# Bias rows copied to DRAM head by head, and SSM constants prepared one stage earlier

## The chip, the cores and the metric

The program runs on one core of one Trainium2 chip. The metric is the device time of the program in microseconds (us), the median of three executions. The core's engines are TensorE (PE, matrix products), VectorE (DVE), ScalarE (ACT) and GpSimd (POOL); SyncE (SP) issues most transfers, ScalarE issues some, and sixteen DMA engines carry them all.

## The reference, cut to what matters

Two residual networks run one after the other on 256 tokens of width 2048, everything in 32-bit floats. The first has two layers: a latent attention (MLA) with its output projection, and a sliding-window attention (SWA) with its output projection. The second mixes an attention with eight heads and a state-space model (SSM), and ends in a feed-forward part.

Two things in it belong to this change. The attention of the second network adds a bias that depends only on the distance between query and key:

```
bias_h = rel_bias.T
lg_own = einsum('bhqd,bhtd->bhqt', qc, k_own) * scale + bias_h[:, t5_bucket(rel_own)]
```

The SSM uses a time step for each of its sixteen heads, projected from the layer's input and passed through a softplus, a decay, and a short convolution in front:

```
xbc = silu(causal_depthwise_conv(xbc, conv_w, conv_b))
dt  = softplus(dt_raw + dt_bias)
a   = -exp(a_log)
a_cs = cumsum(dt * a)
```

## The kernel before

The 256 tokens stand on the free axis and the features on the 128 partitions, so the hidden state is sixteen tiles of 128 x 256 (`KT` = 16). Every large weight lies in DRAM in one packed stream, `wst`, in the order of its use, in pieces of 128 x 1024 floats (512 KB). `fetch` (L285) brings the next piece into one of five `raw` buffers through SyncE's queue. `split_w` (L296) turns it into a high part `whi`, rounded on ScalarE, and a remainder `wlo`, computed on VectorE; four buffers hold each.

`proj` (L326) makes one block of 128 output features: 16 pairs of matmuls, one with `whi` against 512 columns (L336) and one with `wlo` against 256 (L339). A block uses two pieces. `out_mla` (L808) and `out_swa` (L906) run sixteen such blocks each (`j` from 0 to 15), add the residual into `x` and split the new `x` into the operands `hl` of the next stage. `paired` (L343) is a smaller product with both parts of the weights side by side: 16 matmuls at L351. `side` (L360) prepares its weights.

`biases` (L695) is called at block 8 of `out_mla`. It loads a constant (`hot`) and the bias table (`rel`), multiplies them (L706), and keeps the result in `row`, eight partitions of 384 floats, one per head. It loads the time-step weights `wdt`. Last, one transfer on ScalarE's queue writes `row` 128 times into the DRAM tensor `biasrows`, whose order is [128 copies, 8 heads, 384]. Much later the attention reads each head's part back with a skewed pattern, 128 x 256 values a head (L1133).

`mix` (L973) follows `out_swa`. It opens the pool `ssm` and makes there the halved convolution weights `cwh` and `cbh`, the zeroed margins of `pads`, the time-step weights `wdts` (by `side`), then runs `paired` on them; later come `ea` (the exponential of `alog`) and two operands, `acs` and `pick`, for spreading sums over partitions.

The order of instructions on each engine is not that of the code. A planner simulates the engines and gives each engine, at each time, the instruction that is ready and stands earliest in the code; an instruction of later code is taken ahead of time when nothing earlier is ready. It also puts in the waits. Within a pool, a tile waits for the tiles that held its memory before. `with self.tc.manual_schedule(...)` fixes the order by hand in a few places, none of them in the stages of this change.

Of the kernel before, what the change touches and what calls it, by code (L numbers as in the profile page):

```python
# [9 lines left out]
F32 = mybir.dt.float32  # L10
F32R = mybir.dt.float32r
I32 = mybir.dt.int32
AF = mybir.ActivationFunctionType
ALU = mybir.AluOpType
# [3 lines left out]
S = 256  # L18
D = 2048
KT = D // 128  # L20
# [207 lines left out]
class _Kernel:  # L228
# [466 lines left out]
    def biases(self, P):  # L695

        nc = self.nc
        n = 384
        at = _CST["hot"][0]
        hot = P.tile([33, n], F32, name="hot")  # L700
        nc.scalar.dma_start(out=hot, in_=self.cst_dram[0:33, at : at + n])
        rel = P.tile([33, 8], F32, name="rel")
        nc.vector.memset(rel, NEG)
        nc.scalar.dma_start(out=rel[0:32, :], in_=self.rel)
        p = self.aux.tile([128, 512], F32, name="m", bufs=2)
        nc.tensor.matmul(p[:8, :n], rel, hot, start=True, stop=True)  # L706
        row = P.tile([8, n], F32, name="bias")
        self.act(row, p[:8, :n])
        self.wdt = self.const.tile([128, 256], F32, name="wdt")
        nc.scalar.dma_start(out=self.wdt, in_=self.wdt_dram)  # L710
        self.bias = self.tc.dram_tile([128, 8, n], F32, name="biasrows")
        nc.scalar.dma_start(out=self.bias.rearrange("i h n -> h i n"),
                            in_=row.unsqueeze(1).to_broadcast([8, 128, n]))

    def mla(self):
        nc, tc = self.nc, self.tc
# [91 lines left out]
    def out_mla(self):  # L808
        nc = self.nc
        self.xp = self.ctx.enter_context(self.pool("x"))  # L810
        self.x, self.xs, ss = [], [], None
        with self.pool("again") as P:
            for j in range(KT):
                if j == 8:
                    self.biases(P)
                if j == KT - 1:
                    self.roots(self.x[-2])
                if j % 4 == 0:
                    x0 = P.tile([128, 4, S], F32, name="x0", bufs=2)
                    nc.sync.dma_start(out=x0, in_=self.xt[:, j : j + 4, :])  # L820
                x = self.new_x(j)
                self.add2(x, self.proj(self.y), x0[:, j % 4, :])
                self.x.append(x)
                self.xs.append(self.split(self.hx, 16, x, self.v("g2", j)))
                ss = self.square(ss, x)
        self.hy.__exit__(None, None, None)
        self.c2 = self.rstd(self.mean(ss), D, self.const.tile([128, 2], F32, name="c2"))
        self.r2 = self.spread(self.c2)
        for j in range(KT):
            self.dump(f"x1_{j}", self.x[j])  # L830
# [75 lines left out]
    def out_swa(self):  # L906
        nc = self.nc
        gfp = self.const.tile([128, KT], F32, name="gfp")
        self.tt(gfp, self.v("gf", 0, KT), self.v("gpre", 0, KT), ALU.mult)
        old, self.x, self.xs, ss, sg = self.x, [], [], None, None  # L910
        for j in range(KT):
            x = self.new_x(j)
            if j == KT - 1:
                self.roots(self.x[-2])
            self.add2(x, self.proj(self.y), old[j])
            self.x.append(x)
            self.xs.append(self.split(self.hx, 16, x, gfp[:, j : j + 1]))
            ss = self.square(ss, x)
            sg = self.square(sg, x, self.v("gf", j))
        for j in range(KT):  # L920
            self.dump(f"x2_{j}", self.x[j])
        self.hy.__exit__(None, None, None)

        cf = self.rstd(self.mean(ss), D)
        q = self.tmp("n4", (128, 2), 1)
        self.tt(q, self.mean(sg), cf, ALU.mult)
        self.tt(q, q, cf, ALU.mult)
        self.c3 = self.rstd(q, D, self.const.tile([128, 2], F32, name="c3"))
        self.tt(self.c3, self.c3, cf, ALU.mult)
        self.r3 = self.spread(self.c3)  # L930
        self.rf = self.spread(cf)

    def normed(self, j):

        self.stt(self.x[j], self.x[j], self.v("gf", j), self.rf, ALU.mult, ALU.mult)
        self.dump(f"x3_{j}", self.x[j])
# [36 lines left out]
    def mix(self):  # L973
        nc, tc = self.nc, self.tc
        xs = self.xs
        ident = self.k("ident")
# [1 line left out]
        self.hy = self.pool("hy3", side="right")  # L978
        hy = self.hy.__enter__()
        with self.pool("ssm") as P:  # L980
            self.cwh = P.tile([128, 48], F32, name="cwh")
            self.cbh = P.tile([128, 12], F32, name="cbh")
            nc.vector.tensor_scalar(self.cwh, self.v("cw", 0, 48), 0.5, None, op0=ALU.mult)
            nc.vector.tensor_scalar(self.cbh, self.v("cb", 0, 12), 0.5, None, op0=ALU.mult)
            self.pads = [P.tile([128, 3 + S], F32, name=f"pad{i}") for i in range(2)]
            for p in self.pads:
                nc.vector.memset(p[:, 0:3], 0.0)

            sp = [P.tile([128, 32], F32, name=f"sp{i}") for i in range(4)]
            ea = P.tile([128, 16], F32, name="ea")  # L990
            dta = P.tile([128, 2, 16], F32, name="dta")
            ds = P.tile([128, 16], F32, name="ds")
            bc = [P.tile([128, S], F32, name=f"bc{j}") for j in range(2)]
# [1 line left out]
            xd = P.tile([128, 8, 64], F32, name="xd")  # L995


            ws = P.tile([128, KT, 48], F32R, name="wdts")
            nc.vector.memset(ws[:, :, 16:32].bitcast(F32), 0.0)
            self.side(ws, self.wdt, 16)  # L1000
            u = self.tmp("ys")
            self.paired(xs, ws, 16, u)
            self.tt(u[:16], u[:16], self.r3[:16], ALU.mult)
            p = self.aux.tile([128, 512], F32, name="m", bufs=2)
            for t in range(2):
# [4 lines left out]
            for t in range(2):  # L1010
                self.tt(dt[:, t, :], p[:, 16 * t : 16 * t + 16], db, ALU.add)
            self.softplus(sp, dt.rearrange("p a b -> p (a b)"))
            self.act(ea, self.v("alog", 0, 16), AF.Exp)
            for t in range(2):
                self.stt(dta[:, t, :], dt[:, t, :], -1.0, ea, ALU.mult, ALU.mult)

            p = self.aux.tile([128, 512], F32, name="m", bufs=2)
# [9 lines left out]
            p = self.aux.tile([128, 512], F32, name="m", bufs=2)  # L1027
# [1 line left out]
                nc.tensor.matmul(p[:16, 128 * t : 128 * t + 128], dta[:, t, :], self.k("tri"),  # L1029
                                 start=(t == 0), stop=(t == 1), skip_group_check=True)  # L1030

            acs = P.tile([128, S], F32R, name="acs")
            pick = P.tile([128, 16], F32R, name="pick")
            for z in (acs, pick):
                nc.vector.memset(z.bitcast(F32), 0.0)
            self.act(acs[:16], p[:16, :S])
            self.tt(acs[32:48], p[:16, :S], acs[:16].bitcast(F32), ALU.subtract)
            for a in (0, 32):
                nc.vector.tensor_copy(pick[a : a + 16], ident[:16, :16])

            bc += [P.tile([128, S], F32, name=f"bc{j}") for j in (2, 3)]
            for j in range(4):
# [3 lines left out]
            for c in range(2):  # L1046
                for g in range(2):
                    p = self.aux.tile([128, 512], F32, name="m", bufs=2)
# [7 lines left out]
            st, cb = [], []  # L1056
            for g in range(2):
                p = self.aux.tile([128, 512], F32, name="m", bufs=2)
# [4 lines left out]
                p = self.aux.tile([128, 512], F32, name="m", bufs=2)  # L1063
# [4 lines left out]
                p = self.aux.tile([128, 512], F32, name="m", bufs=2)  # L1068
# [10 lines left out]
            for i in range(8):  # L1079
                g = i // 4  # L1080
                y = self.aux.tile([128, 512], F32, name="m", bufs=2)
                for e in range(2):
                    h = 2 * i + e
                    rr = slice(64 * e, 64 * e + 64)
                    a = self.aux.tile([128, 512], F32, name="s", bufs=2)
# [26 lines left out]
                if i % 4 == 3:  # L1112
                    r = self.spread(self.rstd(self.mean(ss), 512),
                                    P.tile([128, S], F32, name=f"rg{g}"))
                    for j in range(4 * g, 4 * g + 4):
                        self.tt(ys[j], ys[j], r, ALU.mult)
                        y_ssm.append(self.split(hy, 8, ys[j], self.v("gssm", j)))


        y_att = []  # L1120
# [2 lines left out]
        with self.pool("att") as P:  # L1123
            n = 384
            rv = self.c3
            for g in range(2):
# [3 lines left out]
                for j in range(4):  # L1130
                    h = 4 * g + j
# [232 lines left out]
```

## Time and profile before

| | |
|---|---|
| median of 3 executions | 1859.26 us (1858.11 to 1861.4) |
| the profiled execution, its own time | 1858.8 us |
| its span, from the first to the last instruction | 1857.0 us |
| mean granted clock of TensorE | 0.995 |
| `out_mla`: PE time, about | 275 to 372 us |
| `out_swa`: PE time, about | 620 to 703 us |
| `mix` begins on PE | 706.24 us |

All times of the trace count from the start of the span. The profiled execution has 1.8 us around its span.

### The profile page before, as it was taken

How to read it: one execution, taken by the hardware profiler on the slowest of the kernel's cores; microseconds unless marked ns; L12 is line 12 of the kernel's file. 1: busy time of each engine (PE TensorE's matmuls, PEld its weight loads, DVE VectorE, ACT ScalarE, POOL GpSimd, SP SyncE). 2: the span in 40 equal slices, each digit the busy share in tenths (PEclk: the TensorE clock that was granted, in tenths of full speed). 3: DMA queues.
4: the chain of work that ended last, by engine and by line, in shares of the span. 5: the costliest groups of instructions: out<-in, count | busy, mean ns of one | idle time of the engine just before them, and what ended most of it. 6: DMA issues, size and time to landing. Idle time of an engine off the chain costs nothing.

```text
span 1857.0 us, 27806 instructions
## 1 busy us (share of the span) xinstructions
PE 1828.4 (98%) x10306; PEld 1572.9 (85%) x10306; DVE 1398.4 (75%) x2578; ACT 1030.2 (55%) x1832; POOL 0.2 (0%) x4
## 2 busy tenths in 40 slices
PE   9999999999999999999999989999999999999997
PEld 8999987898888887888888878888888888888886
DVE  8887776787888677977766578888888888855554
ACT  8655554567777655556554565444444444544543
POOL 0000000000000000000000000000000000000000
PEclk9999999999999999999999999999999999999999
DMA  8544456654444454544454645555555555555553
GB/s 291 176 151 157 148 175 184 215 183 150 144 158 150 158 191 138 182 170 152 149 194 140 206 145 174 181 182 190 184 187 188 184 191 182 196 186 187 202 187 120
DMA packets 92556, 326.13 MB, mean 176 GB/s; under 512 B 10339, under 2 KB 12804, under 8 KB 92420
## 3 DMA queue, kind: packets, MB, share of 16 engines
q1 hardware_dynamic: 89568, 320.49, 50.4%
q10 hardware_dynamic: 2852, 3.86, 1.1%
q8 instruction: 81, 1.33, 0.3%
q14 instruction: 55, 0.45, 0.1%
HBM read 320.64 MB, written 3.67 MB: 175 GB/s over the span
## 4 chain that ended last, share of the span: by engine, by line
PE 94%; DMA 2%; DVE 2%; ACT 1%; issue 1%; SPq 0%; DVEq 0%; ACTq 0%
PE acc L336 44%; PE acc L339 23%; PE acc L1264 4%; PE acc L1265 4%; PE acc L1266 4%; DMA biasrows<-bias 2%; PE acc L469 1%; PE acc L470 1%; PE acc L468 1%; PE m L594 1%; PE acc L450 1%; PE acc L451 1%; PE acc L449 1%; PE m L582 1%; PE s L791 1%
## 5 line engine op out<-in xcount | busy, mean ns | idle before, releaser
L336 PE MATMUL acc<-hl,whi 128*128 128x512 f32 x3584 | 1279.3, 398 | 4.1 <-ACT whi L276 4.1
L339 PE MATMUL acc<-hl,wlo 128*128 128x256 f32 x3584 | 1016.5, 284 | 3.7 <-DVE wlo L270 3.7
L276 ACT ACTIVATE whi<-raw 128x1024 fp32r<-128x1024 f32 (+1 forms) x606 | 628.6, 1041 | 670.3 <-PE acc L336 311.8
L270 DVE TENSOR_TENSOR wlo<-raw,whi 128x1024 fp32r<-128x1024 f32 (+1 forms) x606 | 727.0, 1203 | 352.5 <-ACT whi L276 348.8
L336 PEld LDWEIGHTS acc<-hl,whi 128*128 128x128 f32 x3584 | 674.1, 188 | 161.0 <-ACT whi L276 6.0
L339 PEld LDWEIGHTS acc<-hl,wlo 128*128 128x128 f32 x3584 | 673.8, 188 | 11.8 <-DVE wlo L270 5.2
L1265 PE MATMUL acc<-wlo,hl 128*128 128x512 f32 x344 | 136.1, 397 | 0.0
L1266 PE MATMUL acc<-whi,hl 128*128 128x512 f32 x344 | 135.3, 394 | 0.0
L1264 PE MATMUL acc<-whi,hl 128*128 128x512 f32 x344 | 118.2, 396 | 0.0
L273 DVE SCALAR_TENSOR_TENSOR g<-pad,vec,g 128x256 f32<-128x256 f32 x176 | 84.2, 482 | 2.8
L1265 PEld LDWEIGHTS acc<-wlo,hl 128*128 128x128 f32 x344 | 64.7, 188 | 16.0
L1264 PEld LDWEIGHTS acc<-whi,hl 128*128 128x128 f32 x344 | 64.7, 188 | 15.6
L1266 PEld LDWEIGHTS acc<-whi,hl 128*128 128x128 f32 x344 | 64.7, 188 | 15.2
L270 DVE TENSOR_TENSOR u<-acc,u 128x256 f32<-128x256 f32 x182 | 75.7, 418 | 0.4
L276 ACT ACTIVATE u<-acc 128x256 f32<-128x256 f32 x184 | 67.2, 366 | 5.7 <-DVE q L270 2.8
L276 ACT ACTIVATE t<-t,nm 128x128 f32<-128x128 f32 x112 | 49.4, 444 | 2.3 <-DVE nm L545 1.4
L270 DVE TENSOR_TENSOR t<-s,cst 128x384 f32<-128x384 f32 (+1 forms) x64 | 32.8, 520 | 20.0 <-PE s L890 12.8
L469 PE MATMUL acc<-wlo,hl 128*128 128x512 f32 (+1 forms) x128 | 47.1, 368 | 0.0
L470 PE MATMUL acc<-whi,hl 128*128 128x512 f32 (+1 forms) x128 | 47.1, 368 | 0.0
L468 PE MATMUL acc<-whi,hl 128*128 128x512 f32 (+1 forms) x128 | 46.8, 368 | 0.0
L451 PE MATMUL acc<-hl,wlo 128*128 128x256 f32 x160 | 45.7, 285 | 0.0
L449 PE MATMUL acc<-hl,whi 128*128 128x256 f32 x160 | 45.5, 284 | 0.0
(294 smaller groups left out, 1652.7 us busy)
## 6 DMA issues: line engine op xcount, KB each, us to landing
raw<-in_wst_dram SPq DMA_DIRECT2D x593, 512.0 KB, 3.3
x<-in_xt_dram SPq DMA_DIRECT2D x7, 512.0 KB, 6.0
raw<-in_wst_dram SPq DMA_DIRECT2D x8, 256.0 KB, 6.1
biasrows<-bias ACTq DMA_DIRECT2D x1, 1536.0 KB
b<-biasrows ACTq DMA_DIRECT2D x8, 128.0 KB, 2.8
gb<-in_gfpost_dram ACTq DMA_DIRECT2D x2, 512.0 KB, 4.7
out_dram<-f SPq DMA_DIRECT2D x4, 256.0 KB, 2.3
out_dram<-hl SPq DMA_DIRECT2D x4, 256.0 KB, 2.5
```

The lines of the kernel that those rows point to most:

```text
L270: self.nc.vector.tensor_tensor(out=out, in0=a, in1=b, op=op)
L273: self.nc.vector.scalar_tensor_tensor(out=out, in0=a, scalar=s, in1=b, op0=op0, op1=op1)
L276: self.nc.scalar.activation(out, in_, func, **kw)
L336: nc.tensor.matmul(acc.rearrange("p a t -> p (a t)"), hi[:, a : a + 128], xs[k].rearrange("p a t -> p (a t)"), start=(k == 0), stop=False, ...
L339: nc.tensor.matmul(acc[:, 0, :], lo[:, a : a + 128], xs[k][:, 0, :], start=False, stop=(k == n - 1), skip_group_check=True)
L451: nc.tensor.matmul(acc[:, 0, :], lo[:, a : a + 128], x[:, 0, :], start=False, stop=(k == 3))
L468: nc.tensor.matmul(o, xh, hi[:, a : a + n], start=(k == 0), stop=False)
L469: nc.tensor.matmul(o, xh, lo[:, a : a + n], start=False, stop=False)
L470: nc.tensor.matmul(o, xl, hi[:, a : a + n], start=False, stop=(k == last))
L1264: nc.tensor.matmul(o, xh, hi[:, w], start=(k == 0), stop=False)
L1265: nc.tensor.matmul(o, xh, lo[:, w], start=False, stop=False)
L1266: nc.tensor.matmul(o, xl, hi[:, w], start=False, stop=(k == NF - 1))
```

## The change

The transfer that writes `row` to DRAM becomes eight transfers, one for each head, in a function `copies`. `biases` is called at block 3 of `out_mla` instead of 8, and `copies` at blocks 4 to 11. The preparation of `wdts`, `ea`, `cwh`, `cbh`, `pads`, `acs` and `pick` moves out of `mix` into a function `ssm_ready`, which is called at block 5 of `out_swa`; their tiles come from a pool `ready`, opened before the blocks of `out_swa` and closed after the SSM part of `mix`. The arithmetic is the same.

```diff
@@ biases
-        nc.scalar.dma_start(out=self.bias.rearrange("i h n -> h i n"),
-                            in_=row.unsqueeze(1).to_broadcast([8, 128, n]))
+        return row
+
+    def copies(self, row, h):
+        n = row.shape[1]
+        self.nc.scalar.dma_start(out=self.bias[:, h : h + 1, :].rearrange("i h n -> h i n"),
+                                 in_=row[h : h + 1].unsqueeze(1).to_broadcast([1, 128, n]))
@@ out_mla
-                if j == 8:
-                    self.biases(P)
+                if j == 3:
+                    row = self.biases(P)
+                if 4 <= j < 12:
+                    self.copies(row, j - 4)
@@ out_swa
+        self.ready = self.pool("ready")
+        R = self.ready.__enter__()
         for j in range(KT):
+            if j == 5:
+                self.ssm_ready(R)
@@ new function
+    def ssm_ready(self, P):
+        nc = self.nc
+        self.wdts = P.tile([128, KT, 48], F32R, name="wdts")
+        nc.vector.memset(self.wdts[:, :, 16:32].bitcast(F32), 0.0)
+        self.side(self.wdts, self.wdt, 16)
+        self.ea = P.tile([128, 16], F32, name="ea")
+        self.act(self.ea, self.v("alog", 0, 16), AF.Exp)
+        self.cwh = P.tile([128, 48], F32, name="cwh")
+        self.cbh = P.tile([128, 12], F32, name="cbh")
+        nc.vector.tensor_scalar(self.cwh, self.v("cw", 0, 48), 0.5, None, op0=ALU.mult)
+        nc.vector.tensor_scalar(self.cbh, self.v("cb", 0, 12), 0.5, None, op0=ALU.mult)
+        self.pads = [P.tile([128, 3 + S], F32, name=f"pad{i}") for i in range(2)]
+        for p in self.pads:
+            nc.vector.memset(p[:, 0:3], 0.0)
+        self.acs = P.tile([128, S], F32R, name="acs")
+        self.pick = P.tile([128, 16], F32R, name="pick")
+        for z in (self.acs, self.pick):
+            nc.vector.memset(z.bitcast(F32), 0.0)
+        for a in (0, 32):
+            nc.vector.tensor_copy(self.pick[a : a + 16], self.k("ident")[:16, :16])
@@ mix: the same lines leave the pool "ssm"; what stays is
+            ea, acs, pick = self.ea, self.acs, self.pick
...
-            self.paired(xs, ws, 16, u)
+            self.paired(xs, self.wdts, 16, u)
...
+        self.ready.__exit__(None, None, None)
```

## Rows read from the trace of the kernel before

**Rows 1.** The page: busy time, share of the span and instructions of each engine.
```profile
PE 1828.4 (98%) x10306; PEld 1572.9 (85%) x10306; DVE 1398.4 (75%) x2578; ACT 1030.2 (55%) x1832; POOL 0.2 (0%) x4
```
**Rows 2.** Timeline of PE in `out_mla`: start, us, instruction [idle before, releaser].
```profile
295.61 0.39 PE L336 MATMUL acc<-hl,whi 128*128 128x512 f32 x1
295.84 0.28 PE L339 MATMUL acc<-hl,wlo 128*128 128x256 f32 x1
295.96 0.40 PE L336 MATMUL acc<-hl,whi 128*128 128x512 f32 x1
...
299.75 0.51 PE L336 MATMUL acc<-hl,whi 128*128 128x512 f32 x1 [2.93 <-ACT whi L276]
301.01 0.58 PE L339 MATMUL acc<-hl,wlo 128*128 128x256 f32 x1 [0.75 <-DVE wlo L270]
...
303.95 0.44 PE L336 MATMUL acc<-hl,whi 128*128 128x512 f32 x1
...
320.24 0.39 PE L339 MATMUL acc<-hl,wlo 128*128 128x256 f32 x1 [0.68 <-DVE wlo L270]
```
**Rows 3.** Stretches after both stops: length, busy PE PEld DVE ACT POOL, clock, DMA.
```profile
706.20:711.20 5.00, 4.96 (x15) 2.54 (x16) 1.30 (x4) 0.81 (x3) 0.00 (x0) 0.66 0.29 105
...
299.70:303.90 4.20, 3.40 (x10) 2.69 (x11) 3.24 (x5) 2.07 (x4) 0.00 (x0) 0.61 0.81 233
```
**Rows 4.** Timeline of ScalarE and VectorE in `out_mla` around the copy.
```profile
279.83 0.30 ACTq L712 DMA_DIRECT2D biasrows<-bias  x1
...
280.51 1.41 DVE L270 TENSOR_TENSOR x<-acc,x 128x256 f32<-128x256 f32 x4
...
298.64 1.06 ACT L276 ACTIVATE whi<-raw 128x1024 fp32r<-128x1024 f32 x1 [11.35 <-DMA raw<-in_wst_dram]
```
**Rows 5.** DMA, 288 to 292 us: packets, MB, engine share; issues, us to landing.
```profile
q10 hardware_dynamic: 132, 0.20, 46.7%
q1 hardware_dynamic: 57, 0.23, 17.6%
...
raw<-in_wst_dram SPq DMA_DIRECT2D x2, 512.0 KB, 17.0
```
**Rows 6.** DMA, 304 to 308 us.
```profile
q1 hardware_dynamic: 176, 0.63, 38.7%
q10 hardware_dynamic: 119, 0.18, 25.8%
```
**Rows 7.** Timeline at the start of `mix`.
```profile
703.46 0.18 DVE L983 TENSOR_SCALAR cwh<-vec 128x48 f32<-128x48 f32 x1
...
705.68 0.41 DVE L270 TENSOR_TENSOR wdts<-wdt,wdts 128x256 fp32r<-128x256 f32 x1
...
706.24 5.19 PE L351 MATMUL acc<-hl,wdts 128*48 128x512 f32 x15 [3.51 <-DVE wdts L270]
706.38 0.48 DVE L273 SCALAR_TENSOR_TENSOR hl<-x,gfp,hl 128x256 fp32r<-128x256 f32 x1
```
**Rows 8.** The chain that ended last, the same helper in the MLA stage.
```profile
56.90 3.66 PE acc L351 x16
```
**Rows 9.** Stretch before `out_swa`, columns as in rows 3.
```profile
620.00:630.00 10.00, 10.00 (x63) 8.34 (x63) 2.28 (x4) 3.47 (x6) 0.00 (x0) 1.00 0.32 105
```
**Rows 10.** DMA, 1850 to 1857 us: the final stores.
```profile
DMA packets 864, 1.57 MB, mean 225 GB/s; under 512 B 96, under 2 KB 96, under 8 KB 864
...
q1 hardware_dynamic: 864, 1.57, 62.7%
```
**Rows 11.** Transfers of `wdt` and `hot`: duration ns min/median/max, first and last start.
```profile
L710 ACTq DMA_DIRECT2D wdt<-in_wdt_dram x1: 384/384/384, 1.2 to 1.2; - x1
...
L701 ACTq DMA_DIRECT2D hot<-in_cst_dram x1: 558/558/558, 255.6 to 255.6; - x1
```
**Rows 12.** The final stores, second half of them: issue times and landing.
```profile
L1302 SPq DMA_DIRECT2D out_dram<-hl x4: 333/333/333, 1851.5 to 1853.4; - x4
...
DMA to landing us min/median/max: 2.3/2.4/2.6
```

More of the change, by code (lines that the diff above doesn't have):

```diff
@@ L980, in mix @@
         with self.pool("ssm") as P:
[L981 to L987, printed above, removed]
             sp = [P.tile([128, 32], F32, name=f"sp{i}") for i in range(4)]
-            ea = P.tile([128, 16], F32, name="ea")
+            ea, acs, pick = self.ea, self.acs, self.pick
             dta = P.tile([128, 2, 16], F32, name="dta")
@@ L995, in mix @@
             xd = P.tile([128, 8, 64], F32, name="xd")
-            ws = P.tile([128, KT, 48], F32R, name="wdts")
-            nc.vector.memset(ws[:, :, 16:32].bitcast(F32), 0.0)
-            self.side(ws, self.wdt, 16)
             u = self.tmp("ys")
-            self.paired(xs, ws, 16, u)
+            self.paired(xs, self.wdts, 16, u)
             self.tt(u[:16], u[:16], self.r3[:16], ALU.mult)
@@ L1012, in mix @@
             self.softplus(sp, dt.rearrange("p a b -> p (a b)"))
-            self.act(ea, self.v("alog", 0, 16), AF.Exp)
             for t in range(2):
@@ L1030, in mix @@
                                  start=(t == 0), stop=(t == 1), skip_group_check=True)
[L1032 to L1035, printed above, removed]
             self.act(acs[:16], p[:16, :S])
             self.tt(acs[32:48], p[:16, :S], acs[:16].bitcast(F32), ALU.subtract)
-            for a in (0, 32):
-                nc.vector.tensor_copy(pick[a : a + 16], ident[:16, :16])
             bc += [P.tile([128, S], F32, name=f"bc{j}") for j in (2, 3)]
```

## The prediction, made before the result was known

> **What bounds the kernel now.** I read the page first: TensorE (PE) is busy for 98% of the span [rows 1], so an edit gains only where PE waits or runs at a low clock. The timeline of PE then shows two stops that touch this diff, one in `out_mla` [rows 2] and one at the start of `mix` [rows 7].
>
> *The stop in `out_mla`.* A pair of matmuls (L336, then L339 0.23 us later) starts every 0.35 us. The pair due at 296.66 starts at 299.75; its second half comes at 301.01 where 299.98 was due; from there to 303.95, 1.52 us were due (0.12 and four pairs) and 2.94 pass; later one L339 waits 0.68 us [rows 2]. That is 3.09 + 1.03 + 1.42 + 0.68 = 6.2 us. [...] The cause is a copy: `biasrows<-bias` is issued at 279.83, and ScalarE then finds no weights to convert until 298.64 [rows 4]. Between 288 and 292 the copy's queue (q10) holds 47% of the sixteen engines' time, and two weight pieces issued there (q1) take 17 us to land [rows 5].
>
> *The stop at `mix`.* PE idles 3.5 us, until 706.24, because the last `wdts` operand is made only at 705.68 on VectorE, behind other constants [rows 7]. The 15 matmuls L351 that follow take 5.0 us at a granted clock of 0.66 [rows 3]; the same helper's 16 at 56.90 took 3.66 us [rows 8], so 15 should take 3.4. The stop costs 3.5 + 1.6 = 5.1 us.
>
> **The change part by part.** *SSM constants.* Ten VectorE instructions leave the start of `mix`, from `cwh` (0.18) to the `wdts` difference (0.41), with fills and small copies of 0.07 to 0.33 us between [rows 7]: some 1.8 us. Two activations of ScalarE and a table load leave with them. In `out_swa` they lie under PE: just before that stage VectorE is busy for 2.3 of 10 us [rows 9], so they cost nothing there; without that cover, 1.8 us. With `wdts` ready PE goes on at 702.73 (706.24 less 3.51). Late next is the split of `x` 15 (`hl`, done at 706.86 [rows 7]), wanted by the sixteenth matmul at about 702.73 + 3.4 = 706.1; its chain loses up to 1.8 us of work in front of it and should be in time. I take the whole 5.1 us; with `x` 15 where it is, 4.4; if the moved code fills no gap, 0. The chain that ends in `r3` moves up too, so no new wait there.
>
> *The old copy.* Removing it gives back the 6.2 us. Without any copy: 1858.8 (the profiled execution's own time, span 1857.0 plus 1.8; the median shown is 1859.26) - 5.1 - 6.2 = 1847.5 us.
>
> *The new copies, each.* The old copy read eight SBUF partitions, one per head. Its pace hardly depends on what else the engines carry: 132 packets of 1536 bytes in 4 us beside 57 weight packets, 119 beside 176 [rows 5, 6]. That is 46 to 51 GB/s, so one of its own ends sets it. The writing end is not slow in itself: the final stores put 1.57 MB into DRAM with 62.7% of sixteen engines in 7 us [rows 10], 358 GB/s while they run. Each engine there reads one partition at a time, at 358/16 = 22.4 GB/s: the most that one partition is seen to give. A new copy reads one partition for all its 128 packets (196.6 KB). Bounds: 0.5 us at the stores' full rate and 4.0 us at the old copy's 49 GB/s, if neither depends on the partitions read; 32 us if the old pace belongs to each partition (49/8 = 6 GB/s). I take 22.4 GB/s, 8.8 us each, 70 us for eight where the old copy took 34.7: it is the nearest row for reading one partition. [...]
>
> *When they are issued.* `copies` stands at blocks 4 to 11, but the planner lets an instruction go as soon as its inputs exist and its queue is free: `wdt`, written in block 8, is loaded at 1.2 us, `hot` at 255.6 [rows 11]; the old copy of block 8 left at 279.83, before the sums of blocks 0 and 1 at 280.51 [rows 4]. Once the row exists all eight copies are ready, and ScalarE is busy only 55% [rows 1]. I expect the row again just before 279.8 and the copies behind it within some 10 us. Their issue adds 7 x 0.30 us [rows 4] to ScalarE, inside the 11 us in which it waits for weights anyway.
>
> *What they do to the weights.* PE needs 1 MB every 16 pairs x 0.35 = 5.6 us. Under the old copy the pieces behind it on the engines waited with it, and PE lived from its stock until 296.66. Now copies lie on the queues from 280.5 for 70 us, to 350.5. A piece of 512 KB then passes in 1.5 us at 358 GB/s, and PE starts 1.1 us after ScalarE (298.64 to 299.75 [rows 2, 4]): 353.1, or 56.4 us after 296.66. Pieces that slip in between copies shorten this: there are five `raw` buffers, each worth 8 x 0.35 = 2.8 us, so 14 us for one round. 56.4 - 14 = 42.4, plus the 1.42 us of low clock behind the wait: 43.8 us. Bounds: none slips in, 57.8; two rounds slip in, 29.8; copies that hold up nothing, 0.
>
> *Sum.* 1847.5 + 43.8 = **1891 us**; this case alone 1877 to 1905.
>
> **Rivals.** *Cheap copies (faster).* The copy's pace belongs to its split over the engines, not to the partitions: 47% of sixteen engines is 7.5, so the old copy seems to have used eight. If 128 rows spread over sixteen, a copy takes 2 us, eight together 16 us, and PE's stock (296.66 - 280.5 = 16 us) covers it: 1847.5 us. For it: half of the engines never worked on the old copy. Against it: that copy's 1.5 KB packet held an engine for 0.467 x 16 x 4/132 = 0.23 us, where a 2 KB packet of the stores took 0.627 x 16 x 7/768 = 0.09 [rows 5, 10] (768 of the 864 carry data); something shared slows it. It decides below about 2.5 us a copy. [...]
>
> *Copies spread as written.* One per block of 5.6 us. A copy takes 8.8 us and a block's weights (1 MB at 358 GB/s) 2.9. If they add up, eight blocks take 94 us where PE needs 45; less the stock of 16 us, 33 us are lost: 1880. If weights pass wholly beside the copies, 8 x 3.2 - 16 = 10 us: 1857. Middle: 1868. For it: the order of the code. Against it: [rows 11].
>
> *Copies chained.* If each copy waits on ScalarE's queue until the one before has landed, conversions behind it wait too: 70 us plus eight landings of 2.4 us, above 1905 us. Against it: the final stores write stripes of one tensor in the same way and leave 0.65 us apart though each lands after 2.4 [rows 12].
>
> *The second part does nothing* (PE still waits, on `x` 15 or a late `wlo`): up to 5.1 us more in each case.
>
> **How the numbers follow.** Cheap copies 0.17; spread 0.20, of which 0.04 ends under 1855.5 and 0.04 near 1859; the burst that I forecast 0.56; chained or worse 0.07. A measurement of this kernel tells about 0.2%, 3.7 us. Faster: 0.17 + 0.04 = 0.21. Same: 0.04. Slower: 0.12 + 0.56 + 0.07 = 0.75. To leave out no more than 0.2 the range keeps the cheap copies and cuts the chained ones: 1847 to 1905. The likeliest case alone is 1877 to 1905.
>
> **What would show it.** At `mix`: no PE wait for `wdts`, and 15 matmuls L351 in about 3.4 us. In `out_mla`: eight issues on ScalarE within some 10 us of the bias row; q10 at about 15 packets per us (22 GB/s) for over 55 us; weight pieces landing after more than 20 us; PE idle for tens of us from about 297. If q10 moves 60 packets per us or more, the cheap copies were right; if the issues stand 5 us or more apart, the spread. I am wrong above all if one partition feeds sixteen engines faster than 22 GB/s, or if weight packets pass beside waiting copy packets.

## The result, and the profile after

The changed kernel takes 1879.49 us (median of four runs, 1879.12 to 1882.41), the kernel before, run beside it, 1859.33 (1858.11 to 1861.4). The ratio is 1.0116, 95% interval 1.0105 to 1.0128: slower by 20.2 us. The forecast was 1891, slower.

The spans differ by 20.5 us (1877.5 against 1857.0), and one marker splits them. The first matmul L582 after 400 us, the start of the stage behind `out_mla`, begins at 443.3 us; before at 419.4. So 23.9 us are lost in `out_mla`, and 3.4 won after it. The page, first the share of the copies' queue, then the costliest group, with its idle time and what ended it:

```profile
q10 hardware_dynamic: 2972, 3.86, 2.8%
...
L336 PE MATMUL acc<-hl,whi 128*128 128x512 f32 x3584 | 1279.7, 398 | 26.3 <-ACT whi L276 26.3
```

PE waits for `whi`, which ScalarE makes from the weights, for 26.3 us in the whole program. The timeline of PE, its waits between 285 and 345 us (start, us, instruction, idle before, releaser), answers to [rows 2]:

```profile
308.82 0.80 PE L336 MATMUL acc<-hl,whi 128*128 128x512 f32 x1 [17.34 <-ACT whi L276]
322.55 0.80 PE L336 MATMUL acc<-hl,whi 128*128 128x512 f32 x1 [6.18 <-ACT whi L276]
323.81 0.58 PE L339 MATMUL acc<-hl,wlo 128*128 128x256 f32 x1 [0.46 <-DVE wlo L270]
340.78 0.51 PE L336 MATMUL acc<-hl,whi 128*128 128x512 f32 x1 [1.56 <-ACT whi L276]
342.04 0.39 PE L339 MATMUL acc<-hl,wlo 128*128 128x256 f32 x1 [0.76 <-DVE wlo L270]
```

In `out_mla` these are 25.1 us for `whi` and 1.2 for `wlo`. The first stop begins at 291.5 us, 5.2 before the moment at which the old kernel ran dry. The timeline of ScalarE and its DMA issues over that time answers to [rows 4]:

```profile
279.33 0.48 ACT L276 ACTIVATE bias<-m 8x384 f32<-8x384 f32 x1
279.84 0.59 ACTq L717 DMA_DIRECT2D biasrows<-bias  x1
...
280.63 4.92 ACTq L717 DMA_DIRECT2D biasrows<-bias  x2
...
286.07 6.97 ACTq L717 DMA_DIRECT2D biasrows<-bias  x1
...
293.07 14.60 ACTq L717 DMA_DIRECT2D biasrows<-bias  x2
307.72 1.06 ACT L276 ACTIVATE whi<-raw 128x1024 fp32r<-128x1024 f32 x1 [19.64 <-issue]
307.74 6.48 ACTq L717 DMA_DIRECT2D biasrows<-bias  x1
314.27 0.51 ACT L276 ACTIVATE hl<-x,vec 128x256 fp32r<-128x256 f32 x1 [5.50 <-issue]
314.32 7.01 ACTq L717 DMA_DIRECT2D biasrows<-bias  x1
...
321.44 1.06 ACT L276 ACTIVATE whi<-raw 128x1024 fp32r<-128x1024 f32 x1 [6.35 <-issue]
...
339.67 2.25 ACT L276 ACTIVATE whi<-raw 128x1024 fp32r<-128x1024 f32 x2 [8.22 <-DMA raw<-in_wst_dram]
```

The eight issues, 0.3 us each in the forecast, hold ScalarE for 40.6 us (the sum of the rows). From the fourth on an issue takes about 7 us, as long as one copy (eight pass in 56.8 us, 7.1 each), as if the queue took the next copy only when it had done with an earlier one. By the count of the loads, the piece that is converted at 307.72 had landed at 278.6. Read alone, these lines say that PE stops because ScalarE is stuck in its own issues; only the last one has ScalarE waiting for weights, 8.22 us. The DMA view for 290 to 330 us offers another reason; it answers to [rows 5, 6] (packets, MB, share of sixteen engines; then issues, KB each, us to landing):

```profile
q10 hardware_dynamic: 824, 1.14, 82.0%
q1 hardware_dynamic: 734, 2.67, 16.3%
...
raw<-in_wst_dram SPq DMA_DIRECT2D x6, 512.0 KB, 15.2
biasrows<-bias ACTq DMA_DIRECT2D x5, 192.0 KB, 24.9
```

The copies move 1.14 MB in 40 us, 28.5 GB/s, yet hold 82% of the engines: a packet, 1.4 KB in the mean, sits on an engine for 0.82 x 16 x 40/824 = 0.64 us. Weights (q1) get 67 GB/s, where PE needs 1 MB in 5.6 us, 180 GB/s [rows 2]. Two causes fit one stop.

At the start of `mix` the wait is gone. First VectorE in `out_swa`, then PE at `mix`, where [rows 7] had 3.51 us of idle time:

```profile
650.69 0.42 DVE L270 TENSOR_TENSOR wdts<-wdt,wdts 128x256 fp32r<-128x256 f32 x1
```

```profile
726.52 3.40 PE L351 MATMUL acc<-hl,wdts 128*48 128x512 f32 x14
```

### The profile page after: what moved, and what is told of

Same layout as the page of the kernel before. It is cut to its first block, busy times and chain, and to the rows that moved or that the text cites. A ratio compares the mean times of both kernels' runs of the same rounds, so it can differ in the third digit from the quotient of the medians.

```text
span 1877.5 us, 27817 instructions
## 1 busy us (share of the span) xinstructions
PE 1828.6 (97%) x10306; PEld 1573.1 (84%) x10306; DVE 1398.4 (74%) x2578; ACT 1027.7 (55%) x1830; POOL 0.2 (0%) x4
## 4 chain that ended last, share of the span: by engine, by line
PE 93%; DVE 2%; issue 1%; DMA 1%; ACTq 1%; ACT 1%; SPq 0%; DVEq 0%
PE acc L336 43%; PE acc L339 22%; PE acc L1281 4%; PE acc L1283 4%; PE acc L1282 4%; PE acc L468 1%; PE acc L470 1%; PE acc L469 1%; PE m L594 1%; ACTq L717 1%; PE acc L450 1%; PE acc L451 1%; PE acc L449 1%; PE m L582 1%; DMA raw<-in_wst_dram 1%
## 5 line engine op out<-in xcount | busy, mean ns | idle before, releaser
L336 PE MATMUL acc<-hl,whi 128*128 128x512 f32 x3584 | 1279.7, 398 | 26.3 <-ACT whi L276 26.3
## 6 DMA issues: line engine op xcount, KB each, us to landing
biasrows<-bias ACTq DMA_DIRECT2D x8, 192.0 KB, 23.9
```

Of the source, the lines that this page charges most:

```text
L336: nc.tensor.matmul(acc.rearrange("p a t -> p (a t)"), hi[:, a : a + 128], xs[k].rearrange("p a t -> p (a t)"), start=(k == 0), stop=False, ...
```

## The experiments

My theory: a copy that reads one partition is slow at its reading end, keeps the DMA engines occupied while it waits, and the weights behind it come too slowly for PE. Rivals: the eight issues on ScalarE are what costs; or the copy's pace has nothing to do with the partitions read. Each ratio is to runs of the kernel before taken beside that kernel; their medians are 1858.4 to 1859.2 us.

**The parts alone.** The second part alone keeps the single old copy; the first part alone keeps the old `mix`.

> The kernel before with the second part of the change alone (constants and time-step weights made ready in the second output projection; one copy as before). If the stop at the start of the SSM stage costs 5.1 us and nothing else moves: 1854.2 us. If what the trace of the changed kernel shows holds here too (end of the second output projection to the end of the program shorter by 3.3 us, since some is given back later): 1856.0. If the moved work only changes place: 1859.3.

> The kernel before with the first part of the change alone (eight copies from single partitions). If the two parts add up, the first output projection loses 23.8 us as in the changed kernel: 1883 us. If the second part has a share in the loss (or the two hide each other): outside 1881 to 1885.

Second part alone: 1855.05 us, ratio 0.998 (0.9971 to 0.9988), 3.7 us won. First part alone: 1884.31, ratio 1.0137 (1.0122 to 1.0153), 25.6 lost; its marker stands at 443.0, as in the changed kernel. The parts add up within the intervals.

**Is it the partitions? One copy, rows four partitions apart.** The matmul that makes the rows writes them to partitions 0, 4, ... 28 in place of 0 to 7.

```
-        rel = P.tile([33, 8], F32, name="rel")
-        nc.scalar.dma_start(out=rel[0:32, :], in_=self.rel)
+        rel = P.tile([33, 32], F32, name="rel")
+        nc.scalar.dma_start(out=rel[0:32, 0:32:4], in_=self.rel)
...
-                            in_=row.unsqueeze(1).to_broadcast([8, 128, n]))
+                            in_=row[0:32:4].unsqueeze(1).to_broadcast([8, 128, n]))
```

> The kernel before with one thing changed: the eight bias rows stand on partitions 0, 4, ... 28 and not on 0 to 7; still one issue, one row each. If partitions four apart are read side by side where neighbours share one way out, the copy's pace rises from some 50 GB/s to four times that or to the stores' 358 GB/s, the copy lasts 4 to 10 us in place of 34, and the stop of 6.2 us in the first output projection goes: 1853 us. If the pace belongs to the partition or to eight engines, the copy lasts 34 us and the time is 1859.

> The rows four partitions apart, one copy, together with the second part of the change. If both gains stand and add up: 1859.3 less 6.2 less 3.3 = 1849.8 us (1848.0 with the whole 5.1). If the copy's place does not matter: 1856. If the gains overlap, between the two.

1852.35 us, ratio 0.9966 (0.9953 to 0.9978); with the second part 1848.73, 0.9944 (0.9931 to 0.9956). PE has no wait in `out_mla`. The DMA view of the first of the two, 285 to 303 us, in which nearly the whole copy passes:

```profile
q1 hardware_dynamic: 1062, 3.83, 57.6%
q10 hardware_dynamic: 1022, 1.56, 23.6%
```

The same eight partitions' worth of bytes take 18 us, not 34.7, at 87 GB/s, with the weights beside it at 213. A packet holds an engine 0.236 x 16 x 18/1022 = 0.07 us, where neighbours took 0.23. So the pace belongs neither to the single partition nor to the count of partitions; it depends on which partitions are read together (0 to 7: 46 to 51 GB/s [rows 5, 6]; four apart: 87). I had expected 4 to 10 us: the copy shared the engines with the weights, 81% busy together.

**Eight issues, but fast copies.** The changed kernel; each head's row stands on eight partitions four apart, and each of the eight copies reads all of them (`rel` gets 64 columns, filled accordingly).

```
-        self.nc.scalar.dma_start(out=self.bias[:, h : h + 1, :].rearrange("i h n -> h i n"),
-                                 in_=row[h : h + 1].unsqueeze(1).to_broadcast([1, 128, n]))
+        a = 32 * (h // 4) + h % 4
+        self.nc.scalar.dma_start(out=self.bias[:, h, :].rearrange("(c r) n -> c r n", c=8),
+                                 in_=row[a : a + 29 : 4].unsqueeze(1).to_broadcast([8, 16, n]))
```

The edit also divides the written side into eight groups of 16 rows; the bytes and their places in DRAM stay the same.

> The changed kernel, its eight issues on ScalarE kept, but each head's row stands on eight partitions four apart (the matmul writes it there), and each copy reads all eight, 16 rows from each. If the partitions read set the pace and a slow copy is what makes the next issue hold ScalarE, each copy takes 1 to 3 us, each issue about 0.3 to 1 us, PE's stop in the first output projection goes, and the time is 1848 to 1851 us. If eight issues cost ScalarE 5 to 7 us each whatever the copy takes, it stays at 1875 to 1880. If only the row count per copy matters (128 packets of 1.5 KB at 17 per us), also 1875 to 1880.

1848.82 us, ratio 0.9948 (0.9936 to 0.9961). The issues (duration ns min/median/max), and PE, DVE, ACT and DMA for 280 to 300 us (length, busy PE, PEld, DVE, ACT, POOL, clock, DMA share, GB/s):

```profile
L721 ACTq DMA_DIRECT2D biasrows<-bias x8: 671/835/1625, 279.7 to 287.6; - x8
```

```profile
280.00:300.00 20.00, 20.00 (x116) 17.45 (x115) 17.23 (x29) 12.44 (x19) 0.00 (x0) 1.00 0.86 300
```

The same line of the changed kernel, and the one after it:

```profile
280.00:300.00 20.00, 11.48 (x65) 9.73 (x63) 7.30 (x13) 4.49 (x7) 0.00 (x0) 0.90 0.90 72
300.00:320.00 20.00, 7.54 (x31) 6.26 (x31) 2.38 (x4) 1.88 (x3) 0.00 (x0) 0.67 0.98 94
```

Eight copies and eight issues cost nothing as soon as the reading end is wide: PE is busy for all 20 us, at the full clock. The number of issues by itself is not the cause. That an issue takes 0.8 us here and 7 there shows that its length follows the copy's.

**One issue, one partition.** The kernel before, its eight rows side by side on one partition, copied in one issue.

```
...
-                            in_=row.unsqueeze(1).to_broadcast([8, 128, n]))
+                            in_=row.unsqueeze(1).to_broadcast([1, 128, 8 * n]))
```

> The kernel before with its single copy, but with the eight rows side by side on one partition (12 KB), so that one issue reads one partition for all 1.57 MB; eight short matmuls and activations write the row. Against the eight issues it keeps the reading end (one partition) and takes away the number of issues. If the pace is set by the reading end, the copy lasts some 58 to 60 us (26 GB/s); if it then starves the weights, 1874 us or more. If what costs is the number of issues on ScalarE, one issue of 0.3 us leaves the stop near that of the kernel before: 1859 to 1863 us, whatever the copy lasts. If the pace does not depend on the partition read, the copy lasts 34 us as before and the time is 1859.

1900.9 us, ratio 1.0225 (1.021 to 1.0241), the worst of all, with a single issue of 0.58 us. The DMA view, 325 to 375 us (the copy left at 320.8 here), has no row of weights at all:

```profile
q10 hardware_dynamic: 112, 1.38, 98.6%
...
raw<-in_wst_dram SPq DMA_DIRECT2D x3, 512.0 KB, 42.8
```

1.38 MB in 50 us, 28 GB/s in packets of 12 KB, and landing took 59.5 us. ScalarE's waits for weights, 320 to 400 us (us in all, times, longest):

```profile
ACT whi L276 <- DMA raw<-in_wst_dram: 48.6, 2, 48.3
```

Slow copies starve PE without holding ScalarE. The packets are larger here as well, and why no weights at all pass beside them is not shown.

**ScalarE free: copies issued by GpSimd,** in whole rows, half rows and quarter rows (8, 16 and 32 issues).

```
-        self.nc.scalar.dma_start(out=self.bias[:, h : h + 1, :] ...
+        self.nc.gpsimd.dma_start(out=self.bias[:, h : h + 1, :] ...
```

> The changed kernel with its eight copies issued by GpSimd in place of ScalarE. All the same bytes from the same single partitions, but no issue can hold ScalarE. If PE lost its 30 us because ScalarE was held by its own issues (six of 4.9 to 14.6 us, some 41 us), weights are converted as they land and the stop shrinks to that of the old copy or less: 1854 to 1860 us. If PE lost them because weight pieces cannot pass beside copies that read one partition each, ScalarE finds nothing to convert: during some 56 us of copies weights pass at about 70 GB/s (7.5 us a piece of 512 KB, of which PE eats one in 2.8 us), so 7.5 pieces x 2.8 = 21 us of work plus a stock of 16 us stand against 56 us, and PE loses 19 us or more: 1874 to 1890 us, with waits of ScalarE on weight loads in place of waits on its own issues. Either way the copies' queue shows about 17 packets per us.

> The eight copies issued by GpSimd, each in two halves of the row: sixteen issues with half the bytes in a packet. With whole rows GpSimd's queue moved packets of 3 KB (1.18 MB in 371), with as many weight packets beside them (289) at a time of 1888.8 us; ScalarE's queue moved 1.4 KB packets (1.14 MB in 824) with 734 weight packets. If weights get about one packet for each copy packet on the shared engines, halves bring some 17 weight packets per us back in place of 7, and with ScalarE never held the time is 1870 to 1882 us. If the share of weights does not follow the packets, it stays at 1886 to 1892. If ScalarE's hold was most of the loss of the changed kernel, it falls under 1865.

> The eight copies issued by GpSimd, each in four pieces of a quarter row: 32 issues. From whole rows to halves the queue went from 512 to 768 packets in all, the weight packets beside them (290 to 330 us) from 289 to 468, and the time from 1888.8 to 1884.1 us. If weights get 0.8 to 0.9 of a packet for each copy packet, quarters give them about as many as the changed kernel had (734) or more, with ScalarE never held by an issue. If the hold of ScalarE cost the changed kernel nothing of its own (weights were the scarcer), the time is then its 1879 us, within 2. If the hold added to the loss, some 26 us of idle time against the 19 to 21 that missing weights explain, the time is 1871 to 1875. If weights do not follow the packets, 1884 or more.

Whole rows 1888.84 us (1.0161, 1.0148 to 1.0175), halves 1884.07 (1.0137, 1.0122 to 1.0153), quarters 1880.07 (1.0108, 1.0091 to 1.0125). The DMA view for 290 to 330 us, whole rows and then quarters (q0 is GpSimd's queue):

```profile
q0 software_dynamic: 371, 1.18, 93.3%
q1 hardware_dynamic: 289, 1.06, 6.5%
```

```profile
q0 software_dynamic: 657, 1.01, 77.7%
q1 hardware_dynamic: 817, 2.99, 18.3%
```

The copies keep 25 to 30 GB/s whatever the packet; the weights get 0.8 to 1.2 packets for each packet of the copies (289 to 371, halves 468 to 551, 734 to 824 on ScalarE's queue, quarters 817 to 657). These counts include packets of 4 bytes, in the quarters half of the copies' own; without them the four ratios are 0.9, 1.1, 0.9 and 2.2. The expectation for halves missed: 468 packets in 40 us are 12 a us and not 17, and 1884.07 lies between its ranges. So on GpSimd's queue, the more packets the same copies are cut into, the more weights pass, and the time follows: 1888.8, 1884.1, 1880.1. With quarters the weights flow as in the changed kernel, no issue touches ScalarE, and the time is the same within 1 us. ScalarE then waits for weights and not for itself; its waits in the quarters, 275 to 365 us:

```profile
ACT whi L276 <- DMA raw<-in_wst_dram: 46.9, 8, 15.6
```

The rival of the issues would have had it under 1875 and falls. Its own share is not exactly zero for certain: up to 345 us the quarters had brought in 0.96 MB less weights (5.33 against 6.29), worth 1.8 pieces or 5 us of PE, and lost only 0.3 us more at the marker. The hold may thus have cost the changed kernel up to 5 us of its 30; I did not separate that.

The changed kernel has a third wait that none of these runs was made for: six times SyncE issues a weight load only when a copy has landed. SyncE's waits, 275 to 345 us:

```profile
SPq L287 <- DMA biasrows<-bias: 24.0, 6, 11.2
```

The quarters have no such wait in that stretch and lose as much, so the loss does not need it; whether it has a share in the changed kernel's is not shown.

Near one weight packet for each copy packet does not hold for every copy here: beside the 112 packets of 12 KB no weights passed, and the old copy lies on both sides (57 to 132 in [rows 5], 176 to 119 in [rows 6]).

**Copies spread over the blocks,** the order in which the code is written. VectorE writes the rows to a tile `late` with zero times the sum `x` of the block before added, so that a copy can't leave early. First with two such tiles, then with eight.

```
+        late = P.tile([8, n], F32, name="late", bufs=2)
+        self.tt(late[:, S:], row[:, S:], row[:, S:], ALU.max)
+        self.stt(late[:, :S], self.x[-1][0:8, :], 0.0, row[:, :S], ALU.mult, ALU.add)
...
-                                 in_=row[h : h + 1].unsqueeze(1).to_broadcast([1, 128, n]))
+                                 in_=late[h : h + 1].unsqueeze(1).to_broadcast([1, 128, n]))
```

> The changed kernel with each copy tied to its block: VectorE first writes the rows into a tile of their own, adding zero times the sum x of the block before, so a copy cannot leave before that block is done (the values stay the same). This is the order in which the code is written. If a burst of 56 us of copies is what starves PE, copies of 7.2 us every 5.6 us (PE's pace for a block) still take as long in all, 56 us or a little more, but PE's stock is drawn on later and the weights fill the gaps: 1865 to 1878 us. If ScalarE is held only because copies queue up behind each other, issues spread by a block hold it 0.3 to 2 us each and the time falls to 1852 to 1860. If copies queue up anyway, 1879 as before.

> As the spread copies of the run before (each copy tied to the sum x of the block before it), but with eight tiles for the tied rows in place of two, so that VectorE never waits for a copy to land before it writes the next rows (it did so for 38.5 us, and PE waited for it). If starving is what costs, copies of about 7 us every 5.6 us still fill some 56 us in which weights pass at about 70 GB/s where PE needs 180, so PE still loses 10 to 22 us against no copies: 1868 to 1880 us. If ScalarE's hold was what cost, issues a block apart hold it little and the time is 1852 to 1860.

Two tiles: 1879.34 us (1.0113, 1.0099 to 1.0127), but for another reason: VectorE waited 38.5 us for copies to land before it could rewrite a tile, and PE waited for VectorE's `wlo`, not for `whi`. PE's waits, 275 to 365 us:

```profile
PE acc L339 <- DVE wlo L270: 19.1, 5, 4.8
```

So that run tells nothing of the spread. Eight tiles: 1857.92 us, ratio 0.9995 (0.9986 to 1.0005), no change from before. The figure for starvation (1868 to 1880) missed, and the time is inside what the rival named. Is it the shorter hold, or the weights? The DMA view for 279 to 345 us:

```profile
q10 hardware_dynamic: 989, 1.36, 48.1%
q1 hardware_dynamic: 2615, 9.54, 39.0%
```

The same stretch of the changed kernel:

```profile
q10 hardware_dynamic: 1152, 1.57, 67.9%
q1 hardware_dynamic: 1725, 6.29, 24.1%
```

3.25 MB more of weights, 6.2 pieces of 2.8 us, make 17.4 us of work; the marker moved by 18.6. The issues held ScalarE little here (0.5 us each, one 2.3), but the quarters did not hold it at all, and their marker is 24 us behind the kernel before. What differs is that the copies started 14 us later, on a fuller stock, with gaps between them in which weights passed (320 GB/s from 330 to 335 us). My expectation had left these out; how much each of them is worth was not measured.

The marker of all runs puts the loss of `out_mla` in one column; the lowest rows have no wait there. They stand 6.6 to 6.9 us ahead of the kernel before, and the changed kernel is 30.5 behind the second of them, which differs from it only in the partitions and the grouping of its copies:

| kernel | marker, us | time, us |
|---|---|---|
| one copy, eight partitions four apart | 412.5 | 1852.35 |
| eight copies, each from eight partitions four apart | 412.8 | 1848.82 |
| the kernel before: one copy, partitions 0 to 7 | 419.4 | 1859.33 |
| changed, spread, eight tiles | 424.7 | 1857.92 |
| changed kernel | 443.3 | 1879.49 |
| changed, GpSimd, quarters / halves / whole | 443.6 / 446.9 / 453.1 | 1880.07 / 1884.07 / 1888.84 |
| one copy, one partition | 461.2 | 1900.9 |

## Why the prediction was right in its sign and 11.5 us too high

*The old copy's stop, 6.2 us: right.* Without it the marker moves by 6.6 to 6.9 us and the time by 6.4. In the kernel before the granted clock was 0.50 from 301.01 to 303.95 us, the stretch to which 1.42 of the 6.2 us belong.

*The stop at `mix`, 5.1 us: right in place, too large in worth.* PE goes on without a wait and 14 matmuls take 3.40 us, as worked out; measured alone, the part is worth 3.7 (interval 2.2 to 5.4), and 3.4 by the spans. Counted from the start of `mix`, PE idles 0.64 us more after 125 to 150 us and 0.48 more after 375 to 425 than before; that returns 1.1 us. The rest, some 0.6, I did not locate.

*Without any copy cost, 1847.5: right.* Two kernels that have the second part and no stop in `out_mla` take 1848.7 and 1848.8.

*The copies' pace, 22.4 GB/s from the row of the final stores: too low.* That row told what an engine moved there, not what one partition can give. The packets of the eight copies passed from 281.1 to 337.9 us, 56.8 and not 70; one partition gives 25 to 30 GB/s in five kernels. Eight neighbouring partitions together gave 46 to 51 GB/s [rows 5, 6], eight partitions four apart 87 with the weights beside them. That more than eight engines would work on a copy, the premise of the cheap rival, came true as well (82% of sixteen is 13), and it did not help: a packet from one partition held its engine for 0.64 us, one from eight partitions four apart for 0.07.

*"Their issue adds 7 x 0.30 us to ScalarE, inside the 11 us in which it waits for weights anyway": this step failed.* The issues took 40.6 us, stood over 34 us and not 10, and left conversions undone, so PE's stock ended at 291.5 and not 296.66. By the estimate from GpSimd's quarters this may have added up to 5 us to the loss. In kind it is the wait of the rival of chained copies: conversions stood behind issues of about 7 us, which took 0.8 where the copies were fast. It also spoils a sign that the prediction had named: issues 5 us or more apart were to show the spread, and they stand 7 us apart because ScalarE was held.

*What the stop costs, 43.8 us: right mechanism, mis-sized term.* Measured 30.5 (26.3 of it waits). Put into the forecast's own sum: copies 13.2 us shorter, -13.2; stock 5.2 shorter, +5.2; weights beside the copies, 67 GB/s for 56 us, 7.2 pieces or 20 us and not five or 14, -6; low clock and whatever else is no wait, 30.5 - 26.3 = 4.2 and not 1.4, +2.8. That makes 32.6. The 1.42 us of low clock in the forecast are the old copy's; no run shows that term for the new ones by itself, and the granted clock of the changed kernel was 0.67 from 300 to 320 us. So the length of the copies is the larger miss, the pieces that slip in the second; the early stop offset part of both, and that the time lies inside 1877 to 1905, by 2.5 us, is in part luck. The prediction had called itself wrong above all if one partition fed the engines faster than 22 GB/s or if weight packets passed beside the copies: both came true (28 and 67 GB/s), and they are these two misses.

*The rival of the spread, 1868,* had a floor of 1857 for weights that pass beside the copies, and the spread kernel with eight tiles took 1857.92. That they meet is luck: with copies of 7.1 us, as measured, and not 8.8, its sum 8 x 1.5 - 16 leaves no loss at all, and the weights passed only in part (60 GB/s from 300 to 305 us). The planner does not spread them by itself: it put all issues at the first chance, as [rows 11] had said.

## What to carry to other kernels

Before a copy out of SBUF that repeats a few rows, ask how many partitions apart its sources lie: rows from partitions 0 to 7 went at 49 GB/s, one partition's at 28, and eight partitions four apart at 87 with the weights passing beside them; here that layout, put on the kernel before with the second part of the change, is the fastest version (1848.73 us; 1848.82 with eight copies, no different within the noise). A slow copy costs most through what shares the DMA engines with it, so cost the weights that still get through (here, from one partition, between none, beside packets of 12 KB, and 1.2 packets for each of its packets) and not the copy's own length. An instruction that the code places block by block leaves as soon as its inputs exist, unless data ties it to the block.

## What the runs showed that I had not expected

- A DMA issue is not always 0.3 us of ScalarE's time: with three earlier copies unfinished it took up to 7.4, about one copy's length; with two, 0.5 to 4.4. On GpSimd's queue the issue of the same copy took 0.52 us; with half or quarter rows GpSimd waited between issues instead.
- Whole rows on GpSimd's queue made 512 packets, 3 KB in the mean, on ScalarE's 1152 of 1.4 KB, from the same bytes; I had expected the same 17 packets a us on both, and 371 in 40 us are 9. GpSimd's version was 9.4 us slower although it left ScalarE free; cutting the rows into quarters took back 8.8 of that.
- Sixteen engines can be 98.6% busy and move 28 GB/s: here the busy share of the DMA engines says that they are held, not that they move much.
